# One masked block's low parts move from GpSimd to VectorE

## The chip, the cores and the metric

The kernel runs on one core of one Trainium2 chip. The time is the device time of one execution in microseconds (us), and lower is better. The core has a matrix engine (TensorE, PE in the profile, with its weight loads shown apart as PEld), VectorE (DVE), ScalarE (ACT), GpSimd (POOL) and SyncE (SP), which here only issues transfers. Each engine works through its own queue in a fixed order, and waits on semaphores for the others.

## The reference, cut to what matters

The reference is one layer of a token model with 1024 latent tokens and 256 context tokens, width 1024: a modulated input, two attention branches side by side, a gated merge, a layer norm, and a feed-forward part with a second layer norm. The change touches the first branch only, the masked one (branch A, "windowed" in the reference). Its heart, cut:

```
# 8 query heads, 2 key/value heads (4 query heads share one), head size 64
for i in range(8):                       # one block of 128 queries
    keys   = window of 3*128 latent keys around block i, then the 256 context keys
    scores = where(mask, q_blk @ keys.T / 8, -inf)
    m = max(max(scores), sink);  e = exp(scores - m)
    p = e / (sum(e) + exp(sink - m))     # a sink logit for each head in the denominator
    out = p @ values
```

Branch B is the same without mask and sink, over all 1280 keys. Everything is float32. TensorE gets each operand as two parts that it can multiply quickly: a high part (the value rounded to the matrix engine's format) and a low part (what the rounding lost). A product that should be exact to float32 takes several passes over such parts.

## The kernel before, in words

One attention **unit** is one block of 128 queries and one key/value head, thus four query heads. Branch A has 16 units, n = 2i + g with i = 0..7 and g = 0, 1; they are written as (i, g) below. A unit of branch A sees three key blocks of 128 (two at the ends i = 0 and 7) and the two context blocks: five blocks, numbered 0 to 4 (four at the ends).

What one unit does, in order of data:

- scores: for each of the four heads TensorE multiplies the query parts by the keys into a PSUM tile `s` (lines 496, 497, the mask at 528). There are two such tiles in turn. VectorE copies each to `p` with its sign turned and takes the row's extreme in the same instruction (line 545, 128x640, followed by a short read of the accumulator). ScalarE takes the exponential in place (line 547) and its row sum. A one-element cast to `pb` (line 550) follows the fourth head; the transposes wait for it.
- values: for each block TensorE transposes the four heads' 128x128 pieces into a PSUM tile `ptr` (line 604, three such tiles in turn, which the query transposes `qtr`, line 486, and the transposed row sums `str`, line 567, also use). From `ptr` come the high part `pth` and the low part `ptl` in SBUF, four of each in turn. TensorE multiplies both with the values into `av` (lines 627 and 628).
- output: ScalarE copies `av` to a tile of `side` (line 639), GpSimd moves its upper half to `up` (line 640), VectorE or GpSimd adds the halves into `ot` (line 643), and GpSimd scales and splits the result (lines 646, 84, 87). For i below 6 VectorE does line 643, for the last units GpSimd does it.
- queries: two units ahead, GpSimd splits the next query block (`qs`, lines 84 and 87), TensorE transposes it (486), and ScalarE copies it to `q` (489).

Who writes the parts of a block is set by `POOL_LO`, one tuple of block numbers for each branch (line 30). This is the body of `tr_step` inside `value_steps`, from line 609:

```
pooled = n in POOL_LO[self.br] and not last and (self.br or 2 <= 2 * self.i + self.g < 2 * NT - 3)
if pooled:
    rw = side_tile()
    nc.scalar.copy(rw, tr)                         # line 612
    split(rw, hi, lo, nc.gpsimd, nc.gpsimd)        # lines 84 and 87
else:
    nc.scalar.copy(hi, tr)                         # line 615
    nc.vector.tensor_tensor(out=lo, in0=tr, in1=hi.bitcast(F32), op=ALU.subtract)   # line 616
```

A pooled block thus goes from PSUM to one of two `side` tiles by ScalarE, and GpSimd makes both parts from there; the `ptr` tile is free once ScalarE has copied it. A block that isn't pooled gets its high part from ScalarE and its low part from VectorE, both read from PSUM; its `ptr` tile is free once VectorE is done. In branch A the condition takes the units n = 2 to 12, eleven units, with block 3 of each.

A second place depends on it: the products of a block are queued in `avq` with a due count, `clk[0] + LAG[self.br] + (PLAG[self.br] if pl else 0)`, so that a pooled block of branch A is asked for one step later than another (`PLAG[0]` is 1).

The score, value and output steps of three neighbouring units are written interleaved. In this part the order of each engine's queue is then set by a scheduler while the program is built, from its own costs, so that the queues aren't in the order of the code. An edit at one place can move instructions around it on all queues.

Of the kernel before, what the change touches and what calls it, by code (L numbers as in the profile page):

```python
# [26 lines left out]
ALPHA = 2.0 ** 0.25  # L27
HALF = 512
FBIG = 3.0e38
POOL_LO = (3,), (2, 6)  # L30
PLAG = 1, 2
VL = 1
NXT = 17
# [36 lines left out]
def layer_kernel(  # L70
# [395 lines left out]
    class Unit:  # L466
# [128 lines left out]
        def value_steps(self):  # L595
# [5 lines left out]
            def tr_step(n):  # L601
# [6 lines left out]
                lo = att.tile([P, 512], R32, tag="ptl", name=f"ptl{nm}_{n}", bufs=4)  # L608
                pooled = n in POOL_LO[self.br] and not last and (self.br or 2 <= 2 * self.i + self.g < 2 * NT - 3)
                if pooled:  # L610
# [1334 lines left out]
```

## Time and profile before

| what | us |
|---|---|
| median of three runs | 1539.09 (1537.86 to 1539.81) |
| time of the profiled execution | 1537.76 |
| span of the profiled execution, first to last instruction | 1536.0 |
| VectorE busy over the span | 1176.7 (77%) |
| ScalarE busy | 788.3 (51%) |
| GpSimd busy | 749.5 (49%) |

Branch A's units fill the stretch from about 340 to 480 us of the span, and branch B's follow to about 735 us. The pooled blocks of branch A are written by GpSimd from 361.5 us (the first) to 450.0 us (the start of the last low part), eleven in all, so that one unit lasts 88.5 / 10 = 8.85 us there.

How to read it: busy times are per engine; durations of neighbouring instructions on one engine overlap by some hundredths of a microsecond, so that the time an engine is taken is better read as the stretch less the idle time shown before its instructions. A matrix instruction's end is modelled, so that a busy TensorE may still be waiting a little inside; the idle time of its weight loads (PEld) shows such waits too, and a little longer than the products' own.

### The profile page before, as it was taken

The numbers are of one execution on the slowest core, as the hardware profiler recorded it, in microseconds if no ns is written. First come the engines' busy times: TensorE is split into PE (matmuls) and PEld (weight loads), VectorE is DVE, ScalarE is ACT, GpSimd is POOL, SyncE is SP. The second block draws the span as 40 slices with busy tenths as digits, with TensorE's granted clock in tenths as the row PEclk, the third lists the DMA queues.
The fourth block names the chain that finished last, engine by engine and source line by source line (L and its number), as shares of the span: only waits on it lengthen the run. The fifth ranks groups of instructions, "written<-read, shape, count | busy, mean of one in ns | idle before, by whom it ended". The sixth has DMA issues, their size and how long they took to land.

```text
span 1536.0 us, 22204 instructions
## 1 busy us (share of the span) xinstructions
PE 1507.2 (98%) x7804; PEld 1263.5 (82%) x7804; DVE 1176.7 (77%) x1761; ACT 788.3 (51%) x1303; POOL 749.5 (49%) x727
## 2 busy tenths in 40 slices
PE   9999999999899999999999999999999999999997
PEld 7888888887777888887888998888888888888887
DVE  6677986638788778878765888888888888657884
ACT  5322222448888777777333554444444444435552
POOL 0356522415667677766123436666667774121121
PEclk9999999999999999999999999999999999999999
DMA  9777672312223677663550322333344447996731
GB/s 371 267 242 247 205 254 87 119 61 70 63 81 82 159 166 154 153 145 87 209 165 24 111 87 96 111 110 110 110 110 110 111 110 229 339 273 210 249 105 55
DMA packets 114399, 232.09 MB, mean 151 GB/s; under 512 B 13200, under 2 KB 28048, under 8 KB 114192
## 3 DMA queue, kind: packets, MB, share of 16 engines
q1 hardware_dynamic: 99056, 201.82, 39.5%
q0 software_dynamic: 10400, 20.19, 8.7%
q10 hardware_dynamic: 4832, 8.68, 1.5%
q8 instruction: 61, 1.00, 0.3%
q14 instruction: 50, 0.41, 0.1%
HBM read 179.45 MB, written 65.86 MB: 160 GB/s over the span
## 4 chain that ended last, share of the span: by engine, by line
PE 88%; POOL 5%; DVE 2%; issue 2%; ACT 2%; DMA 0%; SPq 0%; DVEq 0%; POOLq 0%; ACTq 0%
PE p L90 4%; PE p L91 4%; PE p L92 4%; PE g L90 4%; PE g L91 4%; PE g L92 4%; PE ptr L604 4%; PE av L628 3%; PE av L627 3%; PE b L90 3%; PE b L92 3%; PE b L91 3%; PE c L90 2%; PE c L92 2%; PE d L92 2%; PE c L91 2%
## 5 line engine op out<-in xcount | busy, mean ns | idle before, releaser
L616 DVE TENSOR_TENSOR ptl<-ptr,pth 128x512 fp32r<-128x512 f32 x195 | 128.5, 684 | 28.3 <-ACT pth L615 26.9
L547 ACT ACTIVATE p<-p,nm 128x1280 f32<-128x1280 f32 (+2 forms) x128 | 139.5, 1091 | 12.9 <-DVE p L545 11.9
L615 ACT CAST pth<-ptr 128x512 fp32r<-128x512 f32 x195 | 110.9, 589 | 46.6 <-PE ptr L604 40.3
L87 DVE TENSOR_TENSOR ld<-rd,hd 128x1024 fp32r<-128x1024 f32 x77 | 94.9, 1249 | 51.7 <-ACT hd L82 49.5
L82 ACT CAST hd<-rd 128x1024 fp32r<-128x1024 f32 x77 | 79.4, 1050 | 83.0 <-PE p L92 57.7
L604 PEld LDWEIGHTS ptr<-identr,pb 128*128 128x128 f32 x944 | 97.3, 141 | 21.2 <-ACT pb L550 3.1
L628 PE MATMUL av<-ptl,VT 128*128 128x512 f32 x236 | 98.5, 417 | 10.6 <-POOL ptl L87 10.4
L87 POOL TENSOR_TENSOR wlg<-wg,whg 128x512 fp32r<-128x512 f32 x32 | 48.0, 1510 | 122.2 <-ACT whg L82 83.0
L604 PE MATMUL ptr<-identr,pb 128*128 128x128 f32 x944 | 105.2, 243 | 1.8 <-ACT pb L550 1.2
L90 PE MATMUL p<-hd 128*128 128x512 f32 x264 | 103.5, 392 | 0.0
L627 PE MATMUL av<-pth,VT 128*128 128x512 f32 x236 | 102.2, 433 | 1.2 <-ACT side L639 0.8
L91 PE MATMUL p<-ld,hd 128*128 128x512 f32 x264 | 102.9, 390 | 0.0
L92 PE MATMUL p<-hd,ld 128*128 128x512 f32 x264 | 102.8, 389 | 0.0
L90 PE MATMUL g<-hh,whg 128*128 128x512 f32 x256 | 99.9, 390 | 0.0
L92 PE MATMUL g<-hh,wlg 128*128 128x512 f32 x256 | 99.7, 389 | 0.0
L91 PE MATMUL g<-hl,whg 128*128 128x512 f32 x256 | 99.7, 389 | 0.0
L545 DVE TENSOR_SCALAR_CACHE_REDUCE p<-s,cvt,nmc 128x1024 f32<-128x1024 f32 x64 | 84.0, 1315 | 8.1 <-PE s L497 8.1
L496 PE MATMUL s<-KL,q 128*128 128x512 f32 (+2 forms) x192 | 74.7, 389 | 1.2 <-DVE p L545 1.2
L497 PE MATMUL s<-KL,q 128*128 128x512 f32 (+2 forms) x192 | 72.0, 375 | 0.0
L783 ACT ACTIVATE sg<-g,bgc 128x512 f32<-128x512 f32 x32 | 22.0, 686 | 96.2 <-PE g L92 96.2
L82 ACT CAST wS<-s 128x512 fp32r<-128x512 f32 x76 | 45.3, 620 | 47.5 <-POOL s L1244 46.7
L82 ACT CAST wA<-ru 128x512 fp32r<-128x512 f32 x57 | 35.5, 623 | 63.8 <-PE d L92 34.9
(438 smaller groups left out, 4877.8 us busy)
## 6 DMA issues: line engine op xcount, KB each, us to landing
wml<-in_wmodT_dram SPq DMA_DIRECT2D x48, 512.0 KB
ru<-in_w_up_dram SPq DMA_DIRECT2D x38, 512.0 KB
rd<-td SPq DMA_DIRECT2D x55, 256.0 KB
rd<-sd SPq DMA_DIRECT2D x44, 256.0 KB
rd<-in_w_dn_dram SPq DMA_DIRECT2D x33, 256.0 KB
wm<-in_wmodT_dram SPq DMA_DIRECT2D x16, 512.0 KB
wg<-in_w_g_dram SPq DMA_DIRECT2D x32, 256.0 KB
sgd<-sg ACTq DMA_DIRECT2D x32, 256.0 KB
```

Source lines behind the costliest of these rows:

```text
L82: nc.scalar.copy(hi, src)
L87: lo_eng.tensor_tensor(out=lo, in0=src, in1=hi.bitcast(F32), op=ALU.subtract)
L90: nc.tensor.matmul(ps, a[0], b[0], start=start, stop=False, skip_group_check=resumed)
L91: nc.tensor.matmul(ps, a[0], b[1], start=False, stop=False, skip_group_check=resumed)
L92: nc.tensor.matmul(ps, a[1], b[0], start=False, stop=stop, skip_group_check=resumed)
L545: nc.vector.tensor_scalar(out=out, in0=o, scalar1=self.qscale(nqs)[:, hs] if self.br else -1.0, scalar2=self.other[:, hs], op0=ALU.mult, o ...
L547: nc.scalar.activation(row, row, AF.Exp, bias=self.nm[:, hs], scale=-1.0, accum_out=self.sm[:, hs])
L604: i = nc.tensor.transpose(tr[:, h * P:(h + 1) * P], self.bits[:, h, n * P:(n + 1) * P], identr)
L615: nc.scalar.copy(hi, tr)
L616: nc.vector.tensor_tensor(out=lo, in0=tr, in1=hi.bitcast(F32), op=ALU.subtract)
L627: nc.tensor.matmul(self.av, v, hi, start=first, stop=False)
L628: nc.tensor.matmul(self.av, v, lo, start=False, stop=self.left == 0)
```

## The change

```
-POOL_LO = (3,), (2, 6)
+POOL_LO = (), (2, 6)
```

In branch A no block is pooled any more. For block 3 of the eleven units, ScalarE's copy to `side` (line 612) becomes its cast to `pth` (line 615), VectorE gets a line 616, and GpSimd's lines 84 and 87 for that block go. The due count of these blocks loses its extra step. Branch B keeps its two pooled blocks.

Over the whole program VectorE's queue has 1506 rows in place of 1494 and GpSimd's 672 in place of 694. The queues agree up to the first changed unit and again from the first unit of branch B on. Between these two places the scheduler also gives other orders.

The first place is VectorE's queue in branch A around unit (3,0). `ptl_3_0_4` is the low part of block 4 of unit (3,0), `s_4_0_1` the scores of head 1 of unit (4,0), `sm` the row sums; the number at the end of a name only counts names. Before:

```order
L545 TENSOR_SCALAR p_4_0_3950,nm_4_0_3948<-s_4_0_0_3962,negsink 128x640
L616 TENSOR_TENSOR ptl_3_0_4_3943<-ptr_3_0_4_3937,pth_3_0_4_3942 128x512
L616 TENSOR_TENSOR ptl_3_1_0_3957<-ptr_3_1_0_3951,pth_3_1_0_3956 128x512
L545 TENSOR_SCALAR p_4_0_3950,nm_4_0_3948<-s_4_0_1_3980,negsink 128x640
L616 TENSOR_TENSOR ptl_3_1_1_3977<-ptr_3_1_1_3971,pth_3_1_1_3976 128x512
L545 TENSOR_SCALAR p_4_0_3950,nm_4_0_3948<-s_4_0_2_3988,negsink 128x640
L545 TENSOR_SCALAR p_4_0_3950,nm_4_0_3948<-s_4_0_3_4004,negsink 128x640
L616 TENSOR_TENSOR ptl_3_1_2_4020<-ptr_3_1_2_4014,pth_3_1_2_4019 128x512
L643 TENSOR_TENSOR ot_3_0_4028<-side,up_3_0_4027 64x256 x2
L563 RECIPROCAL sm_4_0_3949<-sm_4_0_3949 128x4
```

With the change:

```order
L545 TENSOR_SCALAR p_4_0_3945,nm_4_0_3943<-s_4_0_0_3957,negsink 128x640
L616 TENSOR_TENSOR ptl_3_0_3_3926<-ptr_3_0_3_3920,pth_3_0_3_3925 128x512
L616 TENSOR_TENSOR ptl_3_0_4_3938<-ptr_3_0_4_3932,pth_3_0_4_3937 128x512
L616 TENSOR_TENSOR ptl_3_1_0_3952<-ptr_3_1_0_3946,pth_3_1_0_3951 128x512
L616 TENSOR_TENSOR ptl_3_1_1_3972<-ptr_3_1_1_3966,pth_3_1_1_3971 128x512
L545 TENSOR_SCALAR p_4_0_3945,nm_4_0_3943<-s_4_0_1_3977,negsink 128x640
L545 TENSOR_SCALAR p_4_0_3945,nm_4_0_3943<-s_4_0_2_3985,negsink 128x640
L616 TENSOR_TENSOR ptl_3_1_2_4017<-ptr_3_1_2_4011,pth_3_1_2_4016 128x512
L545 TENSOR_SCALAR p_4_0_3945,nm_4_0_3943<-s_4_0_3_4001,negsink 128x640
L643 TENSOR_TENSOR ot_3_0_4023<-side,up_3_0_4022 64x256 x2
L616 TENSOR_TENSOR ptl_3_1_3_4051<-ptr_3_1_3_4045,pth_3_1_3_4050 128x512
L616 TENSOR_TENSOR ptl_3_1_4_4063<-ptr_3_1_4_4057,pth_3_1_4_4062 128x512
```

The low part of block 3 comes in directly behind the first head's scores, and four low parts now stand between the first and the second head's scores where two stood; the low part of block 3 of unit (3,1) stands behind the additions of `ot`.

The second place is TensorE's queue where block 3 of unit (3,0) is multiplied (`av`), with the transposes of unit (3,1) and the scores of unit (4,0) around it. Before:

```order
L528 MATMUL s_4_0_2_3988<-maskr,identr 128x2x128
L496 MATMUL s_4_0_2_3988<-KC,q_4_0_3793 128x256
L497 MATMUL s_4_0_2_3988<-KC,q_4_0_3794 128x256
L567 MATMUL str_3_1_3996<-ident,sm_3_1_3823 4x128
L627 MATMUL av_3_0_3934<-pth_3_0_3_3929,VT_2139 128x512
L604 MATMUL ptr_3_1_2_4014<-identr,pb_3_1_3886 128x128 x4
L628 MATMUL av_3_0_3934<-ptl_3_0_3_3930,VT_2139 128x512
L627 MATMUL av_3_0_3934<-pth_3_0_4_3942,VT_2139 128x512
L496 MATMUL s_4_0_3_4004<-KL_2130,q_4_0_3793 128x384
```

With the change:

```order
L627 MATMUL av_3_0_3929<-pth_3_0_3_3925,VT_2139 128x512
L604 MATMUL ptr_3_1_0_3946<-identr,pb_3_1_3884 128x128 x4
L528 MATMUL s_4_0_1_3977<-maskr,identr 128x2x128
L496 MATMUL s_4_0_1_3977<-KC,q_4_0_3790 128x256
L497 MATMUL s_4_0_1_3977<-KC,q_4_0_3791 128x256
L496 MATMUL s_4_0_2_3985<-KL_2130,q_4_0_3790 128x384
L497 MATMUL s_4_0_2_3985<-KL_2130,q_4_0_3791 128x384
L528 MATMUL s_4_0_2_3985<-maskr,identr 128x2x128
L496 MATMUL s_4_0_2_3985<-KC,q_4_0_3790 128x256
L604 MATMUL ptr_3_1_1_3966<-identr,pb_3_1_3884 128x128 x4
L628 MATMUL av_3_0_3929<-ptl_3_0_3_3926,VT_2139 128x512
```

The product with the low part of block 3 stood behind the third head's scores, the transposed row sums and the transposes of the next unit's block 2. It now stands ahead of the row sums, directly behind the transposes of the next unit's block 1, and the product with the high part stands ten rows ahead of it in the queue.

## The prediction

> **What bounds the kernel now.** I read the busy times and costliest groups first, to see which engine sets the end, then the stretch in which the changed blocks are written, and there the waits and the timeline.
>
> ```profile
> PE 1507.2 (98%) x7804; PEld 1263.5 (82%) x7804; DVE 1176.7 (77%) x1761; ACT 788.3 (51%) x1303; POOL 749.5 (49%) x727
> L628 PE MATMUL av<-ptl,VT 128*128 128x512 f32 x236 | 98.5, 417 | 10.6 <-POOL ptl L87 10.4
> ```
>
> TensorE is busy over nearly the whole span, and one group of its products has an idle time worth naming: those that read a low part written by GpSimd. The same waits in the stretch of branch A, as TensorE's weight loads show them, are these:
>
> ```profile
> PEld av L628 <- POOL ptl L87: 12.6, 11, 1.7
> PEld av L627 <- ACT side L639: 3.2, 10, 1.0
> PEld ptr L604 <- ACT pb L550: 0.9, 2, 0.7
> ```
>
> Eleven waits, one in each unit with a pooled block, 12.6 us together, 12.6 / 11 = 1.15 us each. The low parts that cause them:
>
> ```profile
> L616 DVE TENSOR_TENSOR ptl<-ptr,pth x69: 658/685/693, 341.1 to 479.5; 128x512 fp32r<-128x512 f32 x69
> L87 POOL TENSOR_TENSOR ptl<-side,pth x11: 1263/1272/1289, 361.5 to 450.0; 128x512 fp32r<-128x512 f32 x11
> ```
>
> From 361.5 to 450.0 us lie ten unit periods of 88.5 / 10 = 8.85 us. How full the engines are there, and in the neighbours (columns: stretch, length, busy time of PE, PEld, DVE, ACT, POOL, granted clock, transfers):
>
> ```profile
> 361.50:450.05 88.55, 78.91 (x550) 69.19 (x551) 70.93 (x152) 72.20 (x173) 58.90 (x91) 1.00 0.24 63
> 450.05:480.00 29.95, 28.19 (x184) 22.93 (x183) 24.92 (x56) 25.69 (x56) 20.98 (x34) 1.00 0.32 94
> 480.00:735.00 255.00, 253.47 (x1549) 207.82 (x1548) 203.29 (x395) 182.84 (x317) 175.62 (x219) 1.00 0.59 139
> ```
>
> In the first stretch TensorE is idle for 9.6 us, and nothing else is full: VectorE and ScalarE are taken to about 80%. In branch B TensorE is full. So the units of branch A run at the pace of a loop through several queues. One turn of it, unit (3,1):
>
> ```profile
> 402.75 0.59 ACT L612 COPY side<-ptr 128x512 f32<-128x512 f32 x1
> 402.96 0.74 POOL L646 TENSOR_TENSOR ot<-ot,rb 128x256 f32<-128x256 f32 x1
> 403.78 0.41 POOL L84 TENSOR_SCALAR O<-ot 128x256 fp32r<-128x256 f32 x1
> 404.27 0.73 POOL L87 TENSOR_TENSOR O<-ot,O 128x256 fp32r<-128x256 f32 x1
> 404.97 0.62 POOL L84 TENSOR_SCALAR pth<-side 128x512 fp32r<-128x512 f32 x1
> 405.67 1.27 POOL L87 TENSOR_TENSOR ptl<-side,pth 128x512 fp32r<-128x512 f32 x1
> 407.00 0.18 PEld L628 LDWEIGHTS av<-ptl,VT 128*128 128x128 f32 x1 [1.17 <-POOL ptl L87]
> 408.12 0.59 ACT L615 CAST pth<-ptr 128x512 fp32r<-128x512 f32 x1 [1.91 <-PE ptr L604]
> 408.74 0.69 DVE L616 TENSOR_TENSOR ptl<-ptr,pth 128x512 fp32r<-128x512 f32 x1 [0.59 <-ACT pth L615]
> ```
>
> ScalarE has copied block 3 by 403.34. GpSimd first finishes the output of the unit before and takes up the block at 404.97; TensorE gets the low part at 407.00. The transposes of the next unit are queued behind this product, so ScalarE then waits for them (1.91 us) and VectorE for ScalarE (0.59 us). The chain of waits shows GpSimd's part of the loop as well:
>
> ```profile
> 360.85 0.58 POOL pth L84
> 361.50 1.28 POOL ptl L87
> 362.83 0.50 PE av L628
> ```
>
> **The change part by part.** *Removed from GpSimd:* 0.62 + 1.27 = 1.89 us in each of eleven units, 20.8 us of its own time, and worth something only through the wait above: 12.6 us if nothing takes its place.
>
> *ScalarE:* one copy becomes one cast of the same tile, at no cost by these two rows of 361.5 to 450.05:
>
> ```profile
> L615 ACT CAST pth<-ptr 128x512 fp32r<-128x512 f32 x41 | 23.3, 594 | 14.4 <-PE ptr L604 12.5 <-POOL ptl L87 1.8
> L612 ACT COPY side<-ptr 128x512 f32<-128x512 f32 x10 | 5.9, 593 | 0.0
> ```
>
> *Added to VectorE:* one low part for each unit. The duration is 0.685 us, but neighbours overlap:
>
> ```profile
> 404.66 1.88 DVE L616 TENSOR_TENSOR ptl<-ptr,pth 128x512 fp32r<-128x512 f32 x3
> 406.46 0.87 DVE L545 TENSOR_SCALAR_CACHE_REDUCE p<-s,negsink 128x640 f32<-128x640 f32 x1
> ```
>
> Three take 406.46 - 404.66 = 1.80 us of the queue, 0.60 each, so 11 x 0.60 = 6.6 us. VectorE is not the engine that sets the end before, but it becomes the fullest. Its rows in 361.5 to 450.05 (busy, mean ns of one, then idle time before):
>
> ```profile
> L545 DVE TENSOR_SCALAR_CACHE_REDUCE p<-s,negsink 128x640 f32<-128x640 f32 x39 | 33.8, 879 | 9.5 <-PE s L497 9.5
> L616 DVE TENSOR_TENSOR ptl<-ptr,pth 128x512 fp32r<-128x512 f32 x41 | 26.9, 683 | 5.7 <-ACT pth L615 5.7
> L643 DVE TENSOR_TENSOR ot<-side,up 64x256 f32<-64x256 f32 x20 | 11.1, 554 | 2.1 <-POOL up L640 1.8
> ```
>
> Idle 9.5 + 5.7 + 2.1 and 0.3 in smaller groups make 17.6 us, 1.76 a unit; VectorE is taken for 8.85 - 1.76 = 7.09 us a unit, and with one more low part for 7.09 + 0.60 = 7.69. A unit can't be shorter, whatever happens to the waits. That bounds the gain at 8.85 - 7.69 = 1.16 us a unit, 11 x 1.16 = 12.8 us, which nearly equals the wait removed.
>
> How much of VectorE's idle time stays? The waits for scores (0.95 a unit) and for high parts (0.57) are mostly those behind the stalled TensorE, as the timeline above shows, and go with the stall. The wait for `up` (0.18) stays. Following the new order of VectorE's queue through three units with the spacings above (0.80 for a score row, 0.60 for a low part, about 1 us for the two additions of `ot`), I find its next input ready nearly everywhere; the exception, about 0.45 us in one unit of three, is where ScalarE's fourth exponential and the `pb` cast come late for the next transposes. That is 0.15 a unit. With 0.07 for what such a walk misses, 0.4 us of idle time stays: the period becomes 7.69 + 0.4 = 8.09, the gain 0.76 x 11 = 8.4 us. The walk is an estimate from these rows.
>
> *The PSUM tile of block 3* is now free only after VectorE's low part, no longer after ScalarE's copy. The tile is the one that the transposes of the next unit's block 1 take (seven uses of three tiles for each unit), and in the new order these stand directly ahead of the product that waits for the same low part. So the hold adds no wait of its own as long as that low part is early; if it is late, all queued behind them is late: that product, the row sums, block 4, the next transposes, and through them ScalarE's casts. Bounds: nothing, to the whole of the idle time that I let go (third rival). I take nothing.
>
> *GpSimd and VectorE side by side.* The additions of `ot` read two SBUF tiles, and took 0.42 us or twice that:
>
> ```profile
> L643 DVE TENSOR_TENSOR ot<-side,up x20: 418/418/873, 367.2 to 446.6; 64x256 f32<-64x256 f32 x20
> ```
>
> With GpSimd's order changed they could all be short (20 x (0.554 - 0.418) = 2.7 us gained) or all long (20 x (0.873 - 0.554) = 6.4 us lost) of VectorE's time. I take no change, since `up` and the query splits stay on GpSimd around them. The new low parts read one operand from PSUM, and the 69 rows of that kind above stay between 658 and 693 ns while GpSimd is two thirds busy. The Trainium skill's page "SBUF — State Buffer", section "Who interferes with whom", states that a VectorE instruction with two SBUF inputs contends with a GpSimd instruction that reads SBUF, and that one with a single SBUF input does not. By that rule the added work isn't slowed and the additions may be; both rows above agree.
>
> *Due count and order.* The eleven products are asked for one step earlier; what that does is in the new order above. At the end of the branch the order moves too: in 450.05 to 480 TensorE is idle for 29.95 - 28.19 = 1.8 us, which bounds this on both sides; I take nothing. From branch B on the queues are as before and TensorE is full, so what is gained in branch A stays gained.
>
> *The sum:* 1537.76 (the profiled execution; 1.8 us of it lie outside its span) - 8.4 = 1529.4. The median of the runs is 1539.09, 1.3 us above that execution, so the median comes to 1530.7.
>
> **The rivals.** *First, VectorE is always fed:* no idle time beyond the bound, 12.8 us gained, 1526.3. For it: the loop through GpSimd is gone, and the ten units' score waits sit behind its stall. Against: ScalarE is taken for 7.2 of 8.85 us (72.20 over ten units in the stretch above), little less than VectorE, and three queues in fixed order seldom fit without a gap.
>
> *Second, the wait changes its name:* TensorE waits at the same product for VectorE's low part, which queues behind scores and other low parts where GpSimd's queue was half empty. If 1.1 of VectorE's 1.76 us of idle time stays, the period is 8.8 us and the time 1537.76 + 1.3 - 0.6 = 1538.5, no change to be told. For it: up to four low parts now stand in a row between two heads' scores; against: the pooled low part was ready 3.6 us after ScalarE's copy (403.34 to 406.94), and two or three rows of VectorE's queue are 1.2 to 2 us.
>
> *Third, slower: the held PSUM tile.* TensorE's transposes for the next unit wait for VectorE, which waits for ScalarE, which waits for those transposes; VectorE then keeps all its idle time and has 0.60 us more to do. The period is 7.69 + 1.76 = 9.45, the loss 0.60 x 11 = 6.6 us, the median 1545.7. It decides from the point where more than 8.85 - 7.69 = 1.16 us of idle time a unit stay. For it: only three such tiles, shared with row sums and queries. Against: among TensorE's three longest waits above none is one for such a tile. The Trainium skill's "Perfetto Trace Analysis", section "Optimizing Scalar/DVE Operations", leans this way: where VectorE is saturated, it says, offloading even to GpSimd may make sense, and the change takes such an offload back. No row here shows VectorE saturated before the change; after it, 7.69 of 8.09 us comes close.
>
> **How the numbers follow.** Forecast 0.52, first rival 0.16, second 0.17, third 0.15. A difference of 0.2% (3.1 us) is about what a measurement of this kernel can tell from no change: faster means under 1536.0, slower over 1542.2. Forecast and first rival are faster but for the forecast's weak end (0.03), and of the second 0.03 is faster and 0.02 slower; of the third 0.01 can't be told. So faster 0.49 + 0.16 + 0.03 = 0.68, same 0.03 + 0.12 + 0.01 = 0.16, slower 0.02 + 0.14 = 0.16. The forecast's own range is 1526 to 1536; both kinds of outcome are open, so the range reaches from the bound, with a little for the additions of `ot`, 1525.5, to 1540.5, through the second rival; about 0.15 lies above and 0.04 below.
>
> **What would show it.** Right: no wait of a product for GpSimd before branch B; the wait of line 628 for VectorE under 0.3 us a unit; VectorE taken for 7.6 to 7.8 us of a period of 7.9 to 8.3; ScalarE's wait for transposes well under 1.25 us a unit. Wrong: line 628 or line 604 waiting for VectorE's low parts about 1 us a unit (second and third rivals), the additions of `ot` at 0.87 us throughout, or the gain lost in branch B.

## The result, and the profile after

| | before | changed |
|---|---|---|
| median, us | 1539.09 (1537.86 to 1539.81) | 1528.37 (1526.50 to 1529.69) |
| ratio, with its 95% interval | | 0.993 (0.9913 to 0.9947) |
| profiled execution, us | 1537.76 | 1529.58 |
| its span, us | 1536.0 | 1527.8 |

The change makes the kernel 10.7 us faster; 8.4 were forecast (1530.7 us), and the time lies inside the range given. On the page of the kernel before, the shares of the chain of work that ended last are, by engine:

```profile
PE 88%; POOL 5%; DVE 2%; issue 2%; ACT 2%; DMA 0%; SPq 0%; DVEq 0%; POOLq 0%; ACTq 0%
```

On the page of the changed kernel the totals, the chain's shares, and the products that read a low part (line 628) read:

```profile
PE 1508.2 (99%) x7804; PEld 1265.5 (83%) x7804; DVE 1179.8 (77%) x1772; ACT 787.7 (52%) x1303; POOL 729.8 (48%) x705
...
PE 92%; DVE 2%; ACT 2%; issue 1%; POOL 1%; DMA 1%; SPq 0%; DVEq 0%; ACTq 0%; POOLq 0%
...
L628 PE MATMUL av<-ptl,VT 128*128 128x512 f32 x236 | 98.3, 417 | 0.8 <-POOL ptl L87 0.6
```

GpSimd's share of the chain has gone from 5% to 1% and TensorE's has grown from 88% to 92%. The idle time ahead of the products of line 628 has gone from 10.6 to 0.8 us, and what is left lies in branch B.

Where the time came from is read between two fixed points of the program: the transposed row sums of the unit (0,1) (line 567) and those of branch B's first unit. The windows of this stretch, first of the kernel before, then of the changed one (columns: stretch, length, busy time of PE, PEld, DVE, ACT, POOL, granted clock, transfers):

```profile
349.61:481.03 131.42, 119.58 (x822) 102.69 (x821) 107.37 (x232) 109.16 (x254) 88.90 (x138) 1.00 0.27 71
```

```profile
351.17:471.33 120.16, 117.06 (x822) 101.51 (x821) 110.19 (x243) 108.75 (x254) 67.07 (x116) 1.00 0.30 78
```

The same 822 matrix instructions take 11.3 us less, at the same granted clock of 1.00, and all of the gain is here. The two profiled executions differ by 8.2 us alone, since the later one reaches the stretch 1.6 us later (351.17 against 349.61) and takes 1.5 us more behind it: 1527.8 - 471.33 = 1056.5 against 1536.0 - 481.03 = 1055.0. That code is the same in both. In the experiments that leave branch B as it is, this part took 1054.6 to 1056.5 us, so 1.5 us there is within what one execution differs from another.

What the weight loads of TensorE still wait for in branch A, longest first, is short, and names neither GpSimd nor a low part:

```profile
PEld ptr L604 <- ACT rb L573: 1.9, 5, 0.6
PEld ptr L604 <- ACT pb L550: 1.8, 6, 0.8
PEld qtr L486 <- ACT rb L573: 1.5, 5, 0.3
PEld av L627 <- ACT side L639: 1.3, 2, 1.0
```

For VectorE a stretch is taken that begins and ends with its own work: ten units, from the additions of `ot` of unit (0,1)'s output to those ten units on. VectorE's groups in it, before (busy, mean ns of one, idle time before):

```profile
L545 DVE TENSOR_SCALAR_CACHE_REDUCE p<-s,negsink 128x640 f32<-128x640 f32 x41 | 35.6, 879 | 10.1 <-PE s L497 9.5 <-PE ptr L604 0.6
L616 DVE TENSOR_TENSOR ptl<-ptr,pth 128x512 fp32r<-128x512 f32 x41 | 26.9, 683 | 5.7 <-ACT pth L615 5.7
L643 DVE TENSOR_TENSOR ot<-side,up 64x256 f32<-64x256 f32 x20 | 10.7, 536 | 1.7 <-POOL up L640 1.5
```

and after:

```profile
L545 DVE TENSOR_SCALAR_CACHE_REDUCE p<-s,negsink 128x640 f32<-128x640 f32 x41 | 35.2, 877 | 1.7 <-PE s L497 0.7 <-PE ptr L604 0.5
L616 DVE TENSOR_TENSOR ptl<-ptr,pth 128x512 fp32r<-128x512 f32 x51 | 33.7, 687 | 1.9 <-ACT pth L615 1.3
L643 DVE TENSOR_TENSOR ot<-side,up 64x256 f32<-64x256 f32 x20 | 8.8, 442 | 0.1
```

The lengths of the two stretches, and VectorE's busy time in them, third of the busy columns (before, then after):

```profile
357.12:446.19 89.07, 79.47 (x554) 69.42 (x554) 71.00 (x154) 72.74 (x174) 59.14 (x91) 1.00 0.24 63
```

```profile
358.69:436.97 78.28, 77.38 (x560) 68.70 (x559) 73.88 (x162) 72.51 (x174) 40.29 (x72) 1.00 0.28 72
```

A unit went from 8.91 to 7.83 us. VectorE is idle for 78.28 - 73.88 = 4.4 us in ten units instead of 18.1, and taken for 73.88 instead of 71.00. TensorE is busy for 77.38 of 78.28 us.

### The profile page after: what moved, and what is told of

It reads as the page before. It is cut to its first block, busy times and chain, and to the rows that moved or that the text cites. A ratio compares the mean times of both kernels' runs of the same rounds, so it can differ in the third digit from the quotient of the medians.

```text
span 1527.8 us, 22207 instructions
## 1 busy us (share of the span) xinstructions
PE 1508.2 (99%) x7804; PEld 1265.5 (83%) x7804; DVE 1179.8 (77%) x1772; ACT 787.7 (52%) x1303; POOL 729.8 (48%) x705
## 4 chain that ended last, share of the span: by engine, by line
PE 92%; DVE 2%; ACT 2%; issue 1%; POOL 1%; DMA 1%; SPq 0%; DVEq 0%; ACTq 0%; POOLq 0%
PE ptr L604 5%; PE p L90 4%; PE p L92 4%; PE p L91 4%; PE g L90 4%; PE g L91 4%; PE g L92 4%; PE av L627 4%; PE av L628 3%; PE b L90 3%; PE b L91 3%; PE b L92 3%; PE s L497 3%; PE s L496 3%; PE c L90 2%; PE d L90 2%
## 5 line engine op out<-in xcount | busy, mean ns | idle before, releaser
L616 DVE TENSOR_TENSOR ptl<-ptr,pth 128x512 fp32r<-128x512 f32 x206 | 136.4, 687 | 25.8 <-ACT pth L615 23.7
L615 ACT CAST pth<-ptr 128x512 fp32r<-128x512 f32 x206 | 117.2, 587 | 39.1 <-PE ptr L604 33.8
```

## Experiments

Ratios are against the kernel before on the same chip (its medians there were 1539.11, 1539.31 and 1539.22 us). "The stretch" is the one between the two fixed points above: 131.4 us before, 120.2 changed.

**The changed kernel again**, for the runs beside it.

> The changed kernel once more, beside the others on one chip. Both theories: about 1528 us (ratio 0.993), and about 120 us of the span between the transposed row sums of unit (0,1) and those of the first unit of branch B (131.4 us in the kernel before, 120.2 in the changed one).

Measured: 1527.85 us, 0.9924 (0.9909 to 0.9939); the stretch 120.1 us. In the later group of runs:

> The changed kernel beside the next three on one chip: about 1528 us, 120 us for the stretch of branch A.

Measured: 1527.58 us, 0.9925 (0.9913 to 0.9938); the stretch 120.05 us. The gain stands at 11.3 and 11.7 us.

**The product asked for later**, on the kernel before; GpSimd keeps the block:

```
-PLAG = 1, 2
+PLAG = 2, 2
```

> Block 3 stays with GpSimd, but its product is asked for one more step later (the extra count of branch A 2 in place of 1). Theory 1 (TensorE's wait for the late low part is what the time went to; VectorE has only to stay under the period): the wait of line 628 for GpSimd falls from 12.6 us to under 4 us, and the stretch of branch A shortens by 6 to 11 us without any work added to VectorE, so 1529 to 1533 us. Theory 2 (GpSimd's queue with its 1.9 us for each block sets the pace; a later product only moves the wait): under 3 us gained, 1536 us or more, with waits for GpSimd at other lines.

Measured: 1533.48 us, 0.9962 (0.9947 to 0.9977); the stretch 125.3 us, so 6.1 of the 11.3 us, with GpSimd's work as it was and none added to VectorE. That is the first theory's wait and stretch; the time lies 0.5 us above its range. The longest wait of VectorE in branch A of this kernel, and then waits of the weight loads:

```profile
DVE ot L643 <- POOL up L640: 11.2, 10, 1.8
```

```profile
PEld str L567 <- DVE ptl L616: 4.3, 4, 1.3
...
PEld ptr L604 <- DVE ptl L616: 2.0, 3, 1.4
...
PEld av L628 <- POOL ptl L87: 0.7, 2, 0.5
```

The product's wait for GpSimd is cured (12.6 to 0.7 us), and half of what it was worth comes back under other names. VectorE's additions now wait 11.2 us for GpSimd's `up` (2.6 before), and TensorE waits for VectorE. In the last units of the branch `up` stands directly behind the block's low part in GpSimd's queue. So with the product out of the way, GpSimd's queue holds up the units at a second place.

**Five of eleven units taken from GpSimd**, on the kernel before; only units with g = 0 stay pooled:

```
-pooled = n in POOL_LO[self.br] and not last and (self.br or 2 <= 2 * self.i + self.g < 2 * NT - 3)
+pooled = n in POOL_LO[self.br] and not last and (self.br or 2 <= 2 * self.i + self.g < 2 * NT - 3 and self.g == 0)
```

> Only the six units n = 2, 4, .. 12 keep block 3 on GpSimd, five don't. Theory 1 (each unit pays its own wait): five elevenths of the gain in the stretch of branch A, 5/11 x 11.3 = 5.1 us, so about 1534 us; six waits of about 1.15 us remain. Theory 3 (the gain is that of another order of the queues over the whole branch, found once GpSimd is out of the loop everywhere): under 2 us gained, or nearly all of 11 us.

Measured: 1529.83 us, 0.9938 (0.9923 to 0.9953); the stretch 122.4 us. If each pooled unit paid by itself, 5/11 of 11.3 = 5.1 us would be gained; 9.0 were, nearer to the other theory, that of another order of the queues. In the six units that stay pooled only two waits for GpSimd's parts are worth naming:

```profile
PEld av L628 <- POOL ptl L87: 1.3, 2, 1.2
```

GpSimd is hardly earlier there. In these six units its low part is ready 3.1 to 3.2 us after ScalarE's copy, and in the eleven units of the kernel before after 2.6 to 3.6 us, 3.26 on average. What has changed, from the second of the six units on, is how much work TensorE finds in its queue between the block's transposes and that product. Two such stretches, the first in the kernel before, unit (3,1), the second here:

```profile
402.61:407.00 4.39, 3.53 (x26) 3.01 (x25) 3.59 (x8) 3.37 (x9) 3.97 (x6) 1.00 0.32 69
```

```profile
388.66:392.69 4.03, 4.03 (x27) 3.73 (x26) 4.02 (x9) 4.03 (x11) 3.78 (x6) 1.00 0.22 69
```

Before, TensorE is busy for 3.53 of 4.39 us (3.1 of 4.0 on average over the eleven units); here it is busy for all of the 4.03 us and finds the low part written. So the price of 1.15 us a unit belongs to one order of the queues, and the scheduler gave another one once every other unit was free. The trace of this kernel holds a second thing, VectorE's additions:

```profile
L643 DVE TENSOR_TENSOR ot<-side,up x22: 409/420/1429, 357.1 to 439.1; 64x256 f32<-64x256 f32 x22
```

Some take 1.43 us where 0.42 is usual. We come back to it below.

**GpSimd's part shortened, not removed**, on the kernel before: for branch A ScalarE writes both the copy and the high part from PSUM, and GpSimd only the low part.

```
 nc.scalar.copy(rw, tr)
-split(rw, hi, lo, nc.gpsimd, nc.gpsimd)
+if self.br:
+    split(rw, hi, lo, nc.gpsimd, nc.gpsimd)
+else:
+    nc.scalar.copy(hi, tr)
+    nc.gpsimd.tensor_tensor(out=lo, in0=rw, in1=hi.bitcast(F32), op=ALU.subtract)
```

> In branch A's pooled blocks ScalarE writes the copy for GpSimd and also the high part from PSUM; GpSimd writes the low part alone. GpSimd has 0.62 us a unit less to do ahead of the low part, ScalarE 0.48 us more (7.2 + 0.5 = 7.7 of 8.85 us). Theory 1: the wait falls from 1.15 to about 0.5 us a unit and the period by as much, 0.6 x 11 = 6.8 us, so about 1532 us. Theory 2 (GpSimd's whole time a unit): GpSimd had 30 us idle of 88.5 in the stretch before, so its time alone can't set the pace and less of it gains little by itself: 1537 us or more.

Measured: 1535.92 us, 0.9977 (0.9967 to 0.9987); the stretch 128.5 us, 2.9 gained. Neither theory was met: the first said about 1532 us, the second 1537 or more. Waits in branch A of this kernel (line numbers are four higher from this place on):

```profile
PEld av L632 <- POOL ptl L617: 9.2, 10, 1.5
DVE ot L647 <- POOL up L644: 8.5, 11, 1.1
```

A third less work for GpSimd in a block (0.62 of 1.89 us) takes 3.4 us from the product's wait, and adds 5.9 to that of the additions for `up`. Shortening what GpSimd does for the block keeps the block in the loop. ScalarE has a cast of 0.59 us more to do in each unit here, which this run doesn't tell apart.

**VectorE loaded further**, on the changed kernel: block 3's low part is written twice in the eleven units, the second time with the same values.

```
 nc.vector.tensor_tensor(out=lo, in0=tr, in1=hi.bitcast(F32), op=ALU.subtract)   # line 616
+if n == 3 and not self.br and 2 <= 2 * self.i + self.g < 2 * NT - 3:
+    nc.vector.tensor_tensor(out=lo, in0=tr, in1=hi.bitcast(F32), op=ALU.subtract)   # line 618
```

> The changed kernel, with the low part of block 3 written twice over by VectorE in the eleven units (same values, same tile): 0.60 us more of VectorE's queue a unit. In the changed kernel VectorE is idle for 3.9 us of 78.5 (0.39 a unit) and TensorE for 0.9. Theory A (VectorE is the next bound): nearly all of it shows, 4 to 6.6 us more than the changed kernel, 1532 to 1535 us. Theory B (TensorE is the bound, busy for 77.6 of 78.5 us): VectorE's idle time takes up two thirds, at most 0.21 x 11 = 2.3 us more.

Measured: 1533.44 us, 0.9961 (0.9947 to 0.9974), 5.9 us above the changed kernel beside it, where theory B allowed 2.3; the stretch 125.4 us, 5.4 more. The ten units, between the same two additions of `ot`:

```profile
357.42:441.29 83.87, 81.74 (x561) 69.67 (x560) 78.81 (x172) 74.83 (x175) 40.15 (x72) 1.00 0.26 69
```

The period is 8.39 instead of 7.83, 0.56 more for an instruction of about 0.60 us of queue in each unit; VectorE's busy time grows by 0.49 (78.81 against 73.88 in ten units). VectorE's time goes through nearly one to one, so VectorE is what bounds the changed units. The second writing also holds block 3's own `ptr` tile for longer, which could cost by itself, but the waits speak against that. The weight loads of this kernel show how its lateness reaches TensorE:

```profile
PEld ptr L604 <- DVE ptl L616: 4.5, 9, 0.5
PEld ptr L604 <- ACT pb L550: 4.3, 13, 0.6
```

Transposes wait for a PSUM tile that VectorE still reads. The wait names line 616, in eight units the first one behind the second writing (line 618), so it is the tile of a block after block 3; only 0.2 us of TensorE's waits name line 618. So VectorE's whole queue is late, not one tile. A tile held by VectorE is the third rival's mechanism; it appears once VectorE has 0.6 us more to do.

**The additions of `ot` moved to GpSimd**, on the changed kernel, for all units (`NT` is 8), to use the time that GpSimd now has:

```
-oe = nc.gpsimd if (self.br or self.i >= NT - 2) and not last else nc.vector
+oe = nc.gpsimd if not last else nc.vector
```

> The changed kernel, with the two additions of the output of units with i below 6 on GpSimd in place of VectorE: VectorE has about 0.87 us a unit less (7.46 to 6.6), GpSimd 1.5 us more (3.9 to 5.4 of 7.85). Theory A (VectorE is the bound): the period falls to ScalarE's 7.2 or a little above, 0.3 to 0.6 us a unit, 4 to 8 us less over thirteen units, 1520 to 1524 us. Theory B (TensorE is the bound): at most 0.09 us a unit, so within 1.5 us of the changed kernel.

Measured: 1533.96 us, 0.9968 (0.9957 to 0.998): 6.4 us slower than the changed kernel beside it, a miss for both theories. Waits in branch A of this kernel:

```profile
ACT p L547 <- POOL p L542: 13.6, 11, 1.6
DVE ptl L616 <- ACT pth L615: 11.9, 13, 1.4
DVE sm L563 <- ACT p L547: 7.0, 7, 1.1
PEld ptr L604 <- DVE ptl L616: 5.7, 11, 1.1
```

The first is new. Line 542 puts the sink's column into `p`, on GpSimd, 0.2 us of work, and ScalarE's exponentials read that column. GpSimd's timeline in one unit:

```profile
392.11 1.54 POOL L643 TENSOR_TENSOR ot<-side,up 64x256 f32<-64x256 f32 x2
393.73 0.74 POOL L646 TENSOR_TENSOR ot<-ot,rb 128x256 f32<-128x256 f32 x1
394.56 0.41 POOL L84 TENSOR_SCALAR O<-ot 128x256 fp32r<-128x256 f32 x1
395.05 0.75 POOL L87 TENSOR_TENSOR O<-ot,O 128x256 fp32r<-128x256 f32 x1
395.75 0.21 POOL L542 TENSOR_SCALAR p<-sinkb 128x4 f32<-128x4 f32 x1
```

and ScalarE's next row:

```profile
396.00 0.83 ACT L547 ACTIVATE p<-p,nm 128x641 f32<-128x641 f32 x1 [1.43 <-POOL p L542]
```

The column stands behind the whole output of the unit before, and ScalarE waits 1.43 us for it. GpSimd is busy for 82.5 of 126.9 us in the stretch; what counts is where the short instruction stands in its queue. Three runs test this reading.

**The additions on GpSimd, the sink's column on VectorE**: the edit above, and

```
-nc.gpsimd.tensor_scalar(out=self.p[:, :, n], in0=sinkb[...], scalar1=-1.0, ...)   # line 542
+nc.vector.tensor_scalar(out=self.p[:, :, n], in0=sinkb[...], scalar1=-1.0, ...)
```

> As the kernel with the output's additions on GpSimd, and with the 128x4 sink column of line 542 written by VectorE in place of GpSimd. There ScalarE's exponentials waited 13.6 us for that column. Theory (an instruction on GpSimd costs when another engine's queue waits for it, whatever GpSimd's busy time): with the column gone from GpSimd nothing on the way of the scores waits for it; VectorE is taken for about 6.7 us a unit, ScalarE for 7.2, so the period comes to 7.3 to 7.6 and the time to 1521 to 1525 us. Rival (GpSimd's longer queue makes the outputs late, and with them `av` and TensorE): no faster than the changed kernel, 1528 us or more.

Measured: 1522.79 us, 0.9897 (0.9882 to 0.9912), in the range expected, and 4.8 to 5.6 us below the changed kernel's medians, the fastest kernel here. Its stretch, and ten units of it counted at TensorE's transposed row sums:

```profile
349.89:466.00 116.11, 115.18 (x821) 101.84 (x820) 105.49 (x232) 108.98 (x254) 80.15 (x127) 1.00 0.31 81
361.09:437.73 76.64, 76.37 (x559) 68.97 (x557) 71.10 (x154) 72.50 (x172) 50.72 (x81) 1.00 0.28 72
```

A unit takes 7.66 us, a little over the 7.3 to 7.6 expected, and TensorE is busy for 76.37 of 76.64: by its modelled busy time it is now the bound in branch A too, which no run tests. With the 6.4 us lost without the second edit, the column's place in GpSimd's queue was worth 1533.96 - 1522.79 = 11.2 us there.

**The same with the column on ScalarE:**

```
+nc.scalar.activation(self.p[:, :, n], sinkb[:, self.g * 4:self.g * 4 + 4], AF.Identity, scale=-1.0)
```

> The same with the sink column written by ScalarE (about 0.2 us a unit, 7.4 in all). Theory: faster than the additions on GpSimd alone (1534 us), but slower than with VectorE's sink column by up to 0.2 x 13 = 2.6 us if ScalarE is the fullest engine then: 1523 to 1527 us. Rival: 1528 us or more, as above.

Measured: 1525.97 us, 0.9916 (0.9899 to 0.9932), as expected. The wait for GpSimd is gone here too. It is 3.2 us slower than with the column on VectorE. That ScalarE pays for the instruction fits, as it is busy for 110.4 us of the stretch of 118.1, but nothing else tests it.

**Only the column moved**, to VectorE, on the changed kernel:

> The changed kernel with only the sink column moved from GpSimd to VectorE (about 0.1 us a unit more for VectorE). In the changed kernel ScalarE waits for that column 1.5 us in all, twice. Theory: VectorE is the bound, so 0.1 x 14 = 1.4 us slower, less what the two waits give back: within 1.5 us of the changed kernel.

Measured: 1525.59 us, 0.9914 (0.9899 to 0.9929), 2 to 2.8 us below the changed kernel; it was expected within 1.5 us of it, a miss. The stretch is 118.55 us, 1.6 less than in the changed kernel, and the ten units in it are the same (78.30 us against 78.48, at the row sums). Most of the gain lies at the branch's end. From the last of VectorE's additions to branch B's first row sums the changed kernel takes 34.36 us and this one 1.2 less:

```profile
435.06:468.18 33.12, 32.42 (x217) 26.76 (x216) 29.68 (x70) 30.07 (x67) 21.65 (x35) 1.00 0.34 97
```

The other 0.4 us lie ahead of the ten units (7.12 us against 7.52).

At the branch's end GpSimd does the additions already (i = 6 and 7), and the changed kernel has in that part the wait just met:

```profile
ACT p L547 <- POOL p L542: 1.2, 1, 1.2
```

It is gone in this kernel, but ScalarE waits 1.0 us there for VectorE's scores instead. So the place of the gain is shown, its cause is not: the order of the queues at the end differs too.

**No block on GpSimd in branch B either**, on the changed kernel:

```
-POOL_LO = (), (2, 6)
+POOL_LO = (), ()
```

> The changed kernel, with no block on GpSimd in branch B either: two low parts a unit more for VectorE there, 15 units x 2 x 0.60 = 18 us on 202 busy of 255 us. TensorE is busy for 253.2 of 254.7 us in branch B and waits for GpSimd 0.6 us once. Theory 1 (a pooled block costs only where TensorE waits for it): no gain to be had, within 2 us of the changed kernel, or slower by up to 6 us where VectorE's low parts come late. A rival, that taking GpSimd out of the parts helps by itself: 3 us or more faster.

Measured: 1530.22 us, 0.9942 (0.993 to 0.9955), 2.6 us above the changed kernel beside it. Branch B's stretch of this kernel:

```profile
471.30:725.00 253.70, 250.32 (x1529) 205.10 (x1529) 215.43 (x418) 182.34 (x314) 119.65 (x159) 1.00 0.58 138
```

TensorE is idle for 253.70 - 250.32 = 3.4 us. In a stretch of nearly the same length of the changed kernel, with GpSimd's two blocks, it is idle for less:

```profile
471.30:726.00 254.70, 253.20 (x1539) 207.43 (x1538) 202.41 (x392) 181.49 (x316) 174.56 (x218) 0.99 0.58 138
```

From branch B's first row sums to its last this kernel takes 248.2 us, and all the kernels that keep the two blocks 245.8 to 247.7. So GpSimd's blocks hold TensorE up just once in branch B (line 628 waits 0.6 us, on the page above), and to take them away gains nothing. The edit that is worth 11 us in branch A is no gain in branch B, and by the medians a small loss.

## Why the prediction was right, and where it was off

**The loop through GpSimd bounds branch A: right, with one correction.** Its waits went, and the gain came from the ten units as said: 89.07 - 78.28 = 10.8 us in them. How the loop closes, the prediction didn't say. GpSimd's longest wait in the stretch before is for TensorE:

```profile
POOL qs L84 <- PE qtr L486: 29.3, 13, 2.8
```

It waits for TensorE to be done with the query transposes, then splits the next query, does the output and the block, and only then does TensorE get its low part. The waits weren't eleven separate prices either: five units without GpSimd's block gave 9.0 of 11.3 us, and a later product alone gave 6.1 with GpSimd's work unchanged. So much of the gain can be had by the order of the queues. No run keeps the order fixed while the block moves, so how much of the 11.3 us is GpSimd's work and how much the order stays open. The sum wasn't touched by this, because it went by VectorE's time after the change and not by the wait removed.

**VectorE is the next bound, with 0.4 us of idle time a unit: right, the second part by luck.** The run with the second low part shows that VectorE's time sets the period. Idle time is 0.44 a unit (4.4 us in ten units), but not where it was put: of the 0.40, 0.18 was the wait for `up`, which measured 0.01 (0.1 us in ten units), and the rest, put at 0.22, measured 0.43.

**The step that failed is the size of "taken 7.09, and with one more low part 7.69; a unit can't be shorter".** In the ten units VectorE's taken time rose from 71.00 to 73.88 us, by 2.9 where 10 x 0.60 = 6.0 was forecast, so to 7.39 a unit. The new instructions follow each other at the 0.60 us that was said; the other work shrank by 3.1 us, in two parts.

First, **the additions of `ot`**, for which "no change" was taken between -2.7 and +6.4 us: 20 x (536 - 442 ns) = 1.9 us less. The trace of the kernel before shows what makes them long. One pair, and GpSimd's row beside it:

```profile
401.57 1.30 DVE L643 TENSOR_TENSOR ot<-side,up 64x256 f32<-64x256 f32 x2 [0.23 <-POOL up L640]
401.62 0.97 POOL L87 TENSOR_TENSOR qs<-Q,qs 128x256 fp32r<-128x256 f32 x1
```

A pair in the changed kernel is from VectorE's timeline

```profile
398.12 0.84 DVE L643 TENSOR_TENSOR ot<-side,up 64x256 f32<-64x256 f32 x2
```

and GpSimd's subtraction had run ahead of it, undisturbed:

```profile
396.81 0.74 POOL L87 TENSOR_TENSOR qs<-Q,qs 128x256 fp32r<-128x256 f32 x1
```

Before, five of the ten pairs lay fully beside this subtraction (0.97 us of it) and took 1.30 us, and four met only the sink's column and took 0.85. In the changed kernel one pair meets the subtraction for more than 0.3 us. In the kernel with half the units pooled GpSimd's low parts themselves, 1.35 us long, lie beside the pairs, and there a single addition takes up to 1.43. So the forecast took the wrong value although it named the mechanism: in the kernel before VectorE waited for `up`, and began its additions just as GpSimd went on to the subtraction behind `up` in its queue. With VectorE behind its own work instead, they come later. The order of both queues could have shown that.

Second, **durations ahead of a wait**. A low part lasts 0.685 us, of which the next instruction overlaps 0.085 if it is ready. Ahead of a wait nothing overlaps it, and stretch less idle time counts it as taken; so it is with the other rows. Added up over the ten units from the trace, VectorE's durations overlap by 8.0 us before and by 10.1 after. The new low parts, taken at 0.60 each, account for 1.0 of these 2.1 us; the other 1.1 us are instructions that now follow without a pause (VectorE has 36 pauses of over 0.02 us before and 26 after). The Trainium skill's "Perfetto Trace Analysis", section "Optimizing Scalar/DVE Operations", says of an instruction's fixed access overhead that the profiled latency holds about twice the engine's own time of it, since the half for the write's acknowledgement overlaps with the next instruction. The trace agrees that rows overlap, 0.69 us long at a spacing of 0.60; that it is the write's acknowledgement no run here shows. The two parts, 1.9 and 1.1 us, make 3.0 of the 3.1. The first is seen pair by pair, the second is worked out; neither was tried apart.

**The first rival's bound** (1526.3) was no bound for the same reason: with 7.39 taken, always fed would have been shorter still. The measured period of 7.83 lies between its 7.69 and the forecast's 8.09, with the forecast's idle time.

**The second rival** didn't come about: no product waits for VectorE's low part among the waits above. **The third** didn't either, at this load. Its mechanism exists, as the run with the second low part shows, but the hold is short while VectorE is early, as the step on the held tile said.

**ScalarE's cast at no cost: right.** ScalarE's busy time in the stretch is 108.75 us against 109.16. **The end of the branch, nothing within 1.8 us: right;** from the last additions on 34.36 us against 34.84, a gain of 0.5. **Gain kept in branch B: right**, within the 1.9 us by which executions differ there.

**What would show it.** No product waited for GpSimd before branch B, and ScalarE's wait for transposes in the stretch fell from 14.5 to 6.2 us, as named. VectorE's taken time was to be 7.6 to 7.8 and the period 7.9 to 8.3: both are lower, and this is the failed step.

## What to carry to other kernels

Ask of an engine where its instructions stand in a loop that others wait on, not how busy it is: GpSimd, two thirds busy, cost 11 us through its place ahead of one product, and in another kernel as much through one 0.2 us instruction behind four others in its queue. When a stall goes, the next engine's taken time limits the gain; work it out from the spacing of its instructions when they follow each other, since durations measured around waits and beside a neighbour's reads are too long. A wait has its price in one order of the queues only: half of the units freed gave most of the gain, and a product asked for later gave half of it with nothing moved. So a price "for each unit" is to be tested with half of them, and the cheaper reordering is to be tried first.

## What the runs showed of the hardware that was not expected

- The additions with both operands in SBUF are slowed by GpSimd's two-operand subtractions, and hardly by its small sink's column: pairs beside the column took 0.84 to 0.86 us, and so did nine of ten pairs in the kernel whose only edit to the changed one is the column on VectorE, where nothing of GpSimd's lies beside those nine. The slowing is mutual, and has one pattern in these traces: the one that begins second ends a fixed time after the first. In the kernels before, changed, and half pooled, 17 additions of branch A begin more than 0.01 us after the start of such a subtraction and while it runs, and each ends 0.27 to 0.28 us after it, however long it still ran; an addition takes 0.42 us alone. A query's subtraction that begins beside a running addition ends 0.59 to 0.61 us after that addition, and takes 0.74 alone. In the rows above, the pair ends at 402.87 us and the subtraction at 402.59. By an estimate from these numbers (0.42 - 0.28 and 0.74 - 0.60) the second one has about 0.14 us behind it when the first ends, and does the rest only then; so the pair's 1.30 us are 0.84 and 0.74 less twice 0.14. The Trainium skill's "SBUF — State Buffer", section "Who interferes with whom", names this pair of instructions (a VectorE instruction with two SBUF inputs, and a GpSimd instruction that reads SBUF); the trace agrees for the two-operand subtraction. The Trainium skill's "SBUF — State Buffer", section "Summary: rules for kernel authors", lets the second to issue block fully until the first finishes; the trace agrees but for these 0.14 us.
- The low parts, with one operand in PSUM, stayed the same length in all kernels (657 to 694 ns), as in this row of the changed one, where GpSimd is busy for over half of the stretch:

```profile
L616 DVE TENSOR_TENSOR ptl<-ptr,pth x81: 679/687/694, 341.9 to 470.4; 128x512 fp32r<-128x512 f32 x81
```
